# Gated DeltaNet gates worked out with tokens on the partitions, sums over tokens as TensorE products with masks

## The chip, the cores and the metric

The kernel runs on one core of a Trainium2 chip. The metric is the device time of one execution in microseconds; where several executions are shown, their median counts. A core has TensorE (PE, with its weight loads shown apart as PEld), VectorE (DVE), ScalarE (ACT), GpSimd (POOL) and SyncE (SP), which here issues all DMAs. PE multiplies into PSUM; DVE and ACT read PSUM and SBUF, POOL only SBUF.

## The reference, cut to what matters

A two-layer decoder trunk: layer 0 is a gated DeltaNet, layer 1 an RWKV-7 mixer. The prompt has 16 meta tokens and 1024 prompt tokens; besides it there are 8 sample sequences of 8 tokens. The change is in the gates of layer 0: beta and the log decay g, the cumulative sum of g within a chunk, and what follows from it.

```python
proj = xn @ w_in
qkv, z, b, a = proj[..., :c1], proj[..., c1:c2], proj[..., c2:c3], proj[..., c3:]
...
beta = jax.nn.sigmoid(b)
g = -jnp.exp(a_log.astype(jnp.float32)) * jax.nn.softplus(a + dt_bias)
...
gc = jnp.cumsum(g, axis=-1)
decay = jnp.exp(jnp.where(causal, gc[..., :, None] - gc[..., None, :], -jnp.inf))
...
L = jnp.where(strict, jnp.einsum('nbhik,nbhjk->nbhij', kb, k) * decay, 0.0)
A = L + jnp.eye(chunk, dtype=L.dtype)
sol = lax.linalg.triangular_solve(A, rhs, left_side=True, lower=True, unit_diagonal=True)
...
k_dec = k * jnp.exp(g_last[..., None] - gc)[..., None]
q_dec = q * jnp.exp(gc)[..., None]
...
S = S * jnp.exp(gl_c)[..., None, None] + jnp.einsum('bhck,bhcv->bhkv', kd_c, v_new)
```

There are 16 value heads, so b and a are 16 columns each of the input projection.

## The kernel before

**Tiling.** All 1104 tokens (64 sample tokens, 16 meta, 1024 prompt) go through together, as three segments of 384, 384 and 336 columns (`SEGS`), features on the partitions. For the recurrence, tokens are cut in nine groups of 128 (`tg` 0 to 8; group 0 holds the 8 sample sequences in its first 64 rows and a first prompt piece in its last 64). Products in layer 0 are made of three fp32r products (a high and a low part of each operand, `split` and `dense`); weights are loaded by SP, split by ACT (L87, high part) and POOL (L91, low part).

**Layer 0.** `input_norm` loads x, norms it and transposes it onto the features. `gates` projects b and a (L77, tile `d`, 64 columns of weights of which 32 are used). Then come eight head pairs j = 0 to 7. For each pair the projections run in the order of `ORDER`: k, the z of the pair before (x, y), q, and the two v (v, w). `conv` turns k, q, v into conv outputs: an ACT copy out of PSUM, one ACT tap and three DVE taps (L524), a tanh and a DVE product (L530). `gdn_prep` makes the scores K K^T (PE, tile `fsc`), scales them by the decays and bp (DVE L700 to L710), sends the 32x32 blocks through DRAM (`ltd`, L716) and inverts 72 blocks together on DVE in 31 steps of two instructions (`inverse32`, L571 and L573). `spread` sends the inverse through DRAM (`g_t`, `g_u`) to `T1n` and `TT`; the merges y32, u32, y64, u64 on PE (tiles `rY`, `rU`) put the blocks together. `gdn_recur` then runs over the nine groups.

**The order.** Within layer 0, PE and ACT follow an order written out by hand (`manual_schedule`); DVE, POOL and SP are put in order by a planner that simulates a time line. The hand-written order counts in slots: a slot is half a segment of one projection, 12 products on PE. Slot -24 is the first of dk of pair 0, slots -18 to -13 are dq. `self.at(u, f)` puts f behind the slot that lies before u: an event at -23.4 is issued behind slot -24. For pair 0: loads of E at -18.5 to -18.3, exps of E (ACT) from -16, scores at -15.2, -14.4 and -13.6, spread at -1, merges from 2.5 on. The gates are a generator: its first part (projection) runs ahead of the slots, and each `yield` is continued by one event.

**The gates before** (`gates_open`, `gates`, L317 to L404). Heads lie on partitions, 16 each, tokens along the row: `rows[0:16]` is beta, `rows[32:48]` the cumulative sum gc, `rows[64:80]` the rest of the chunk gd = gc at its end minus gc. Per segment: tanh of b, a plus the bias, |a|, exp (ACT and DVE, 16 lanes). Then over all 1104 columns: Ln, softplus, product with -exp(a_log), and the cumulative sum as a DVE scan (L373) with a mask `sm` that is 0 at the start of each chunk. The differences are three DVE subtractions (L379 to L382). The chunk decays exp(gc at the end) are made on 16 lanes (`egl`), written to DRAM (`dgl`, L387) and read back broadcast to 128 partitions (`eglb`, L388). gc goes to DRAM as `drow[j]` in eight DMAs (L393). Last, nine PE transposes (L74) in three batches bring beta, gc and gd onto token partitions, and DVE (L401, L402) and ACT fill `col`, whose four planes are beta, -gc, exp(gc) and exp(gd). These steps are events at -22.9, -19.4, -16.8, -16.7 and -16.6.

**Who uses them.** `decays` (L643 to L657) loads E (for the scores) and attn (for the outputs): gc of a pair's two heads and three groups, broadcast to 128 partitions, one DMA for each pair, segment and use, 48 in all (L647); POOL masks them (L651), ACT takes the exps with `col[..., 1, ...]` as bias. `gdn_prep`, `gdn_tokens`, `gdn_recur` and the sample steps read `col` and `eglb`.

Of the kernel before, what the change touches and what calls it, by code (L numbers as in the profile page):

```python
# [10 lines left out]
AF = mybir.ActivationFunctionType  # L11
ALU = mybir.AluOpType
# [3 lines left out]
NT = 1104  # L16
# [6 lines left out]
NEG = -1.0e30  # L23
# [13 lines left out]
class Builder:  # L37
# [277 lines left out]


    def gates_open(self, ctx):  # L317
        nc, i = self.nc, self.i
        W = i["gdn_w_in"][0]

        self.col = self.t(self.l0, [128, 9, 4, 16], "gcol")
        self.eglb = self.t(self.l0, [128, 16, 17], "eglb")
        self.bmask4 = self.t(self.l0, [64, 4], "bmask4")
        for g in (0, 1):
            nc.gpsimd.tensor_copy(self.bmask4[32 * g:32 * g + 32], self.bmask[32 * g:32 * g + 32, 4 * g:4 * g + 4])
        gp = self.gatep = ctx.enter_context(self.tc.tile_pool(name="gates", bufs=1, reuse_waits="tile"))
        t = self.t
        al = t(gp, [128, 2], "al")
        wz = t(gp, [128, 8, 64], "wz")
        nc.gpsimd.memset(wz, 0.0)  # L330
        wv = W[:, 6144:6176].rearrange("(k p) m -> p k m", p=128)
        nc.sync.dma_start(wz[:, :, 0:16], wv[:, :, 0:16])
        nc.sync.dma_start(wz[:, :, 32:48], wv[:, :, 16:32])
        rows = t(gp, [96, 1152], "rows")
        nc.vector.memset(rows, 0.0)
        g = t(gp, [48, 1152], "g")
        nc.vector.memset(g[32:48], 0.0)
        sm = t(gp, [48, 1152], "sm")
        nc.vector.memset(sm[32:48], 1.0)
        nc.gpsimd.memset(sm[32:48].rearrange("p (c k) -> p c k", k=128)[:, :, 0:1], 0.0)  # L340
        nc.gpsimd.memset(sm[32:48, 0:72].rearrange("p (c k) -> p c k", k=8)[:, :, 0:1], 0.0)
        self.gate_in = al, wz, rows, g, sm
        nc.sync.dma_start(al[32:48, 0:1], i["gdn_a_log"].rearrange("l h -> h l"))
        nc.sync.dma_start(al[32:48, 1:2], i["gdn_dt_bias"].rearrange("l h -> h l"))

    def gates(self, xh, xl):
        nc, i, t, gp = self.nc, self.i, self.t, self.gatep
        al, wz, rows, g, sm = self.gate_in
        nea = t(gp, [128, 1], "nea")
        self.act(nea[32:48], al[32:48, 0:1], AF.Exp)  # L350
        nc.vector.tensor_scalar(nea[32:48], nea[32:48], -1.0, None, op0=ALU.mult)
        whi = t(gp, [128, 8, 64], "whi2", dt=F32R)
        wlo = t(gp, [128, 8, 64], "wlo2", dt=F32R)
        self.split(wz, whi, wlo)
        w = ([whi[:, 0:4, :], whi[:, 4:8, :]], [wlo[:, 0:4, :], wlo[:, 4:8, :]])
        x = t(gp, [48, NT], "ax")
        y = t(gp, [48, NT], "ay")
        for s, (c0, n) in enumerate(SEGS):
            p = self.dense(w, 64, xh, xl, s)
            b = rows[0:16, c0:c0 + n]  # L360
            self.act(b, p[0:16, 0:n], AF.Tanh, scale=0.5)
            nc.vector.tensor_scalar(b, b, 0.5, 0.5, op0=ALU.mult, op1=ALU.add)
            xa, ya = x[32:48, c0:c0 + n], y[32:48, c0:c0 + n]
            self.act(xa, p[32:48, 0:n], AF.Identity, bias=al[32:48, 1:2])
            nc.vector.scalar_tensor_tensor(ya, xa, -1.0, xa, op0=ALU.mult, op1=ALU.max)
            self.act(ya, ya, AF.Exp, scale=-1.0)
        yield
        xa, ya = x[32:48], y[32:48]
        self.act(ya, ya, AF.Ln, bias=1.0)
        nc.vector.scalar_tensor_tensor(ya, xa, 0.0, ya, op0=ALU.max, op1=ALU.add)  # L370
        nc.vector.tensor_scalar(g[32:48, 0:NT], ya, nea[32:48], None, op0=ALU.mult)
        gc = rows[32:48]
        nc.vector.tensor_tensor_scan(gc, sm[32:48], g[32:48], 0.0, op0=ALU.mult, op1=ALU.add)  # L373
        yield
        gd = rows[64:80]
        c3 = lambda x: x.rearrange("p (c k) -> p c k", k=128)
        c8 = lambda x: x[:, 0:64].rearrange("p (c k) -> p c k", k=8)
        v, v8 = c3(gc), c8(gc)
        nc.vector.tensor_tensor(c3(gd)[:, 1:9], v[:, 1:9, 127:128].broadcast_to([16, 8, 128]), v[:, 1:9], op=ALU.subtract)  # L379
        nc.vector.tensor_tensor(c3(gd)[:, 0:1, 64:128], v[:, 0:1, 127:128].broadcast_to([16, 1, 64]), v[:, 0:1, 64:128],  # L380
                                op=ALU.subtract)
        nc.vector.tensor_tensor(c8(gd), v8[:, :, 7:8].broadcast_to([16, 8, 8]), v8, op=ALU.subtract)  # L382
        egl = t(gp, [48, 17], "egl")
        self.act(egl[32:48, 0:8].unsqueeze(2), v8[:, :, 7:8], AF.Exp)
        self.act(egl[32:48, 8:17].unsqueeze(2), v[:, :, 127:128], AF.Exp)
        dgl = self.dram([16, 17], "dgl")
        nc.sync.dma_start(dgl, egl[32:48])  # L387
        nc.sync.dma_start(self.eglb.rearrange("p h c -> p (h c)"),  # L388
                          dgl.rearrange("(o h) c -> o (h c)", o=1).broadcast_to([128, 272]))

        self.drow = self.dram([8, 9, 2, 128], "drow")
        for j in range(8):
            nc.sync.dma_start(self.drow[j].rearrange("t h k -> h t k"), c3(gc)[2 * j:2 * j + 2])  # L393
        for t3 in range(3):
            yield
            p = self.ps("f", 2)
            for k in range(3):
                self.transpose(p[:, 96 * k:96 * k + 96], rows[:, (3 * t3 + k) * 128:(3 * t3 + k + 1) * 128])
            pv = p[:, 0:288].rearrange("p (k x h) -> p k x h", k=3, h=16)
            c = self.col[:, 3 * t3:3 * t3 + 3]  # L400
            nc.vector.tensor_copy(c[:, :, 0, :], pv[:, :, 0, :])  # L401
            nc.vector.tensor_scalar(c[:, :, 1, :], pv[:, :, 2, :], -1.0, None, op0=ALU.mult)  # L402
# [240 lines left out]
    def decays(self, j, s, pool, tag, bufs):  # L643

        nc = self.nc
        E = self.t(pool, [128, 3, 2, 128], tag, bufs)
        nc.sync.dma_start(E.rearrange("p t h k -> p (t h k)"),  # L647
                          self.drow[j, 3 * s:3 * s + 3].rearrange("(o t) h k -> o (t h k)", o=1).broadcast_to([128, 768]))
        E6 = E.rearrange("p t h k -> p (t h) k")

        nc.gpsimd.affine_select(E6, E6, pattern=[[0, 6], [1, 128]], compare_op=ALU.is_ge, fill=NEG, base=0, channel_multiplier=-1)  # L651
        if s == 0:
            nc.gpsimd.memset(E6[0:64, 0:2, 64:128], NEG)
            for h in (0, 1):
                v = E6[0:64, h, 0:64].rearrange("p (b r) -> p b r", r=8)
                nc.gpsimd.affine_select(v, v, pattern=[[-8, 8], [0, 8]], compare_op=ALU.is_ge, fill=NEG, base=0, channel_multiplier=1)
        return E  # L657
# [263 lines left out]
    def gdn_events(self, G, open_, gate, swap):  # L921

        self.events = {}
        base = [-24]
        for j in range(8):
            base.append(base[j] + 6 * min(len(ORDER[j]), 6))
        first = [9, 43] + [base[j + 1] + 6 for j in range(2, 8)]
        for u in (-22.9, -19.4, -16.8, -16.7, -16.6):
            self.at(u, gate)
        self.at(-13, swap)  # L930
        for j in range(8):
            self.chain_events(j, G, first[j])
            self.front_events(j, G, base[j] if j else -24, first[j], first[j - 1] if j else None, open_)
# [1198 lines left out]
    def layer0(self, top, right, xa, xc):  # L2132
# [265 lines left out]
    def wave(self, zin, first, loaded_, stay, last, pool):  # L2398
# [23 lines left out]
        def norms(s):  # L2422
            x = self.sums_in(s)
            for _ in range(2 + s):
                yield
            yield from self.finish(s, x)

        jobs = [(gates, 32, -4.5, 14), (lambda: out(0, Z), 16, 14, 22), (lambda: out(1, DD), 16, 22, 30),
                (lambda: out(2, Z), 16, 30, 38), (lambda: out(3, DD), 16, 38, 46), (lambda: out(4, Z, None, range(6)), 12, 46, 52), (lambda: out(4, DD, x2, (6, 7)), 4, 52.1, 52.45),
                (lambda: out(5, DD, x2), 16, 52.1, 54.5), (lambda: out(6, DD, x2), 8, 54.6, 56), (lambda: self.finish_last(x2), 1, 56, 57)]  # L2430
# [121 lines left out]
```

## Time and profile before

| | us |
|---|---|
| median of three executions | 2184.01 (2181.36 to 2190.6) |
| the profiled execution | 2190.08 |
| its span | 2188.3 |
| granted TensorE clock, mean | 0.981 |

Which engine is busy when, in 40 slices of 54.7 us each (tenths; 9 is 90% or more), with the granted clock:

```profile
PE   5869899999999999999999999999898999999997
DVE  7967869788887979795334676757968657777755
ACT  5526466656565665656533365664746446777774
POOL 3423333334343333334231352343534344444444
PEclk9979999999999999999999999999999999999999
```

How to read the views used below. The page's first part gives the busy us of each engine, its share of the span and its instructions. A wait row names who waited for whom, the us in total, the number of waits and the longest. A row of a stretch gives start:end, its length, and the busy us of PE, PEld, DVE, ACT and POOL with instruction counts, then the granted clock, the DMA share and GB/s. A row of the time line gives the start, the us, the engine and line, and the operation with output<-input, and in brackets the idle time before it and who ended it. A grouped row gives the instructions of a line with their count, then busy us and mean ns, then the idle time before them. SPq rows are DMA issues.

### The profile page before, as it was taken

What the parts mean: (1) busy time and instruction counts of PE and PEld (TensorE: products, weight loads), DVE (VectorE), ACT (ScalarE), POOL (GpSimd) and SP (SyncE); (2) the same over time, 40 slices, a digit from 0 to 9 for tenths busy, and PEclk for the clock granted to TensorE, in tenths of its full rate; (3) what the DMA queues carried; (4) which work ended last, traced back from release to release, by engine and by line L of the source; (5) the groups of instructions that cost most, each with busy time, mean ns of one, the idle gap of its engine ahead of it and who ended that gap; (6) DMA issues with size and microseconds to landing.
All of it is one profiled execution on the core that took longest, in us unless ns stands there. A gap on an engine that the chain in (4) does not pass through costs nothing. (4 is left out here: it accounts for less than half of the span.)

```text
span 2188.3 us, 54818 instructions
## 1 busy us (share of the span) xinstructions
PE 2048.3 (94%) x20404; PEld 1905.8 (87%) x20404; DVE 1585.8 (72%) x4221; ACT 1290.9 (59%) x3761; POOL 841.2 (38%) x1125
## 2 busy tenths in 40 slices
PE   5869899999999999999999999999898999999997
PEld 5859899999999999998899999888898988888876
DVE  7967869788887979795334676757968657777755
ACT  5526466656565665656533365664746446777774
POOL 3423333334343333334231352343534344444444
PEclk9979999999999999999999999999999999999999
DMA  4423342424333333335345115655565476677764
GB/s 119 119 58 87 90 115 85 116 78 106 96 96 106 105 96 102 98 102 165 97 126 134 61 51 190 215 167 168 168 180 152 119 221 175 181 229 221 239 178 138
DMA packets 430661, 292.65 MB, mean 134 GB/s; under 512 B 147145, under 2 KB 412986, under 8 KB 430394
## 3 DMA queue, kind: packets, MB, share of 16 engines
q1 hardware_dynamic: 430394, 289.14, 46.0%
q8 instruction: 161, 2.64, 0.5%
q14 instruction: 106, 0.87, 0.1%
HBM read 197.68 MB, written 91.37 MB: 132 GB/s over the span
## 5 line engine op out<-in xcount | busy, mean ns | idle before, releaser
L91 POOL TENSOR_TENSOR wlo<-wraw,whi 128x512 fp32r<-128x512 f32 (+1 forms) x246 | 328.5, 1337 | 475.8 <-ACT whi L87 432.1
L77 PE MATMUL d<-xc,whi 128*128 128x384 f32 (+2 forms) x1006 | 279.1, 336 | 0.8 <-DVE xc L313 0.7
L524 DVE SCALAR_TENSOR_TENSOR cvy<-raw,cw,cvy 128x408 f32<-128x408 f32 (+2 forms) x288 | 189.1, 657 | 19.2 <-ACT cvy L63 17.8
L87 ACT CAST whi<-wraw 128x512 fp32r<-128x512 f32 (+1 forms) x246 | 149.9, 612 | 87.2 <-PE d L77 50.0
L77 PEld LDWEIGHTS d<-xc,whi 128*128 128x128 f32 (+1 forms) x1006 | 183.0, 189 | 3.4 <-DVE xc L313 1.1
L77 PE MATMUL d<-xc,wlo 128*128 128x384 f32 (+3 forms) x476 | 157.5, 339 | 3.8 <-POOL wlo L91 3.8
L77 PE MATMUL dz<-xc,whi 128*128 128x384 f32 (+1 forms) x480 | 153.7, 338 | 0.0
L77 PE MATMUL dv<-xc,whi 128*128 128x384 f32 (+1 forms) x480 | 152.2, 337 | 0.0
L77 PE MATMUL d<-xa,whi 128*128 128x384 f32 (+3 forms) x450 | 142.9, 341 | 8.4 <-ACT ev L2352 4.1
L63 ACT ACTIVATE o<-rA,gcol 128x128 f32<-128x128 f32 x128 | 42.2, 367 | 116.2 <-DVE S L903 116.0
L571 DVE TENSOR_TENSOR invtmp<-invA,invT 72x31 f32<-72x31 f32 (+15 forms) x248 | 101.8, 411 | 3.2
L77 PE MATMUL dv<-xa,whi 128*128 128x384 f32 (+1 forms) x288 | 99.0, 344 | 0.0
L77 PE MATMUL dz<-xa,whi 128*128 128x384 f32 (+1 forms) x288 | 98.5, 342 | 0.0
L77 PEld LDWEIGHTS d<-xc,wlo 128*128 128x128 f32 (+1 forms) x476 | 89.2, 189 | 7.9 <-POOL wlo L91 4.9
L77 PEld LDWEIGHTS d<-xa,whi 128*128 128x128 f32 (+1 forms) x450 | 84.3, 190 | 12.9 <-ACT ev L2352 4.4
L573 DVE TENSOR_TENSOR invT<-invT,invtmp 72x31 f32<-72x31 f32 (+15 forms) x248 | 92.7, 374 | 3.3
L77 PEld LDWEIGHTS dz<-xc,whi 128*128 128x128 f32 x480 | 89.3, 188 | 4.6 <-issue 4.5
L77 PEld LDWEIGHTS dv<-xc,whi 128*128 128x128 f32 x480 | 89.1, 188 | 1.4 <-issue 1.4
L77 PE MATMUL d<-xa,wlo 128*128 128x384 f32 (+3 forms) x252 | 84.8, 337 | 2.0 <-POOL wlo L91 2.0
L77 PE MATMUL dq<-xc,whi 128*128 128x384 f32 (+1 forms) x240 | 78.3, 343 | 3.0 <-ACT whi L87 3.0
L77 PE MATMUL dk<-xc,whi 128*128 128x384 f32 (+1 forms) x240 | 78.2, 346 | 0.0
L1333 DVE SCALAR_TENSOR_TENSOR mixs<-xb,pcol,mixs 128x320 f32<-128x320 f32 (+2 forms) x96 | 69.4, 733 | 5.0 <-ACT mixs L63 4.7
(523 smaller groups left out, 6821.9 us busy)
## 6 DMA issues: line engine op xcount, KB each, us to landing
wraw<-in_gdn_w_in SPq DMA_DIRECT2D x96, 256.0 KB
wraw<-in_rwkv_w_rkvz SPq DMA_DIRECT2D x80, 256.0 KB
Sb<-in_state_gdn SPq DMA_DIRECT2D x64, 256.0 KB
sldcak<-cakd SPq DMA_DIRECT2D x24, 576.0 KB
wraw<-in_rwkv_w_o SPq DMA_DIRECT2D x42, 256.0 KB
E<-drow SPq DMA_DIRECT2D x24, 384.0 KB
attn<-drow SPq DMA_DIRECT2D x24, 384.0 KB
wraw<-in_gdn_w_out SPq DMA_DIRECT2D x36, 256.0 KB
```

The costliest lines, as they stand in the source:

```text
L63: return self.nc.scalar.activation(out, in_, func, bias=bias, scale=scale, **kw)
L77: self.nc.tensor.matmul(out, lhsT, rhs, start=start, stop=stop)
L87: nc.scalar.copy(hi, x)
L91: e.tensor_tensor(lo, x, hi.bitcast(F32), op=ALU.subtract)
L524: nc.vector.scalar_tensor_tensor(y[0][:, 0:wd], raw[:, k:k + wd], cw[k], y[0][:, 0:wd], op0=ALU.mult, op1=ALU.add)
L571: nc.vector.tensor_tensor(tmp, A[:, j, j + 1:32].unsqueeze(2).broadcast_to([nb, n, m]), Tv[:, j, 0:m].unsqueeze(1).broadcast_to([nb, n, m] ...
L573: nc.vector.tensor_tensor(Tv[:, j + 1:32, 0:m], Tv[:, j + 1:32, 0:m], tmp, op=ALU.subtract)
L1333: nc.vector.scalar_tensor_tensor(x[:, f:], xb[:, 8 + a + f:8 + b], mu, x[:, f:], op0=ALU.mult, op1=ALU.add)
```

## The change

The gates are worked out with tokens on the partitions. The projection's 48 rows are copied out of PSUM once per segment; nine PE transposes put them on 128 partitions as [128, 9 groups, 48], and all elementwise work runs on [128, 9, 16]. The cumulative sum over a chunk's tokens is a PE product with a 0/1 mask `upto` (one mask for group 0 with its sample blocks, one for groups 1 to 8), the rest of the chunk a product with `past`. The chunk decays come out on all 128 partitions by a product of `ones` with g (for group 0, with g split by `part` into its nine chunks), so `dgl` goes. The DRAM rows `drow` get the layout [9, 16, 128] and are written by two DMAs from transposes of gc; `decays` reads them in three pieces per partition. `al` is loaded broadcast to 128 partitions. The masks are made by POOL at the start. The events of the gates become three, at -23.4, -21.4 and -20.4.

```diff
-        al = t(gp, [128, 2], "al")
+        al = t(gp, [128, 2, 16], "al")
...
-        rows = t(gp, [96, 1152], "rows")
-        nc.vector.memset(rows, 0.0)
-        g = t(gp, [48, 1152], "g")
-        nc.vector.memset(g[32:48], 0.0)
-        sm = t(gp, [48, 1152], "sm")
-        nc.vector.memset(sm[32:48], 1.0)
-        nc.gpsimd.memset(sm[32:48].rearrange("p (c k) -> p c k", k=128)[:, :, 0:1], 0.0)
-        nc.gpsimd.memset(sm[32:48, 0:72].rearrange("p (c k) -> p c k", k=8)[:, :, 0:1], 0.0)
-        self.gate_in = al, wz, rows, g, sm
-        nc.sync.dma_start(al[32:48, 0:1], i["gdn_a_log"].rearrange("l h -> h l"))
-        nc.sync.dma_start(al[32:48, 1:2], i["gdn_dt_bias"].rearrange("l h -> h l"))
+        for x, nm in enumerate(("gdn_a_log", "gdn_dt_bias")):
+            nc.sync.dma_start(al[:, x], i[nm].broadcast_to([128, 16]))
+        rows = t(gp, [48, 1152], "rows")
+        nc.gpsimd.memset(rows[:, NT:1152], NEG)
+
+        upto, past = [t(gp, [128, 128], f"upto{k}") for k in (0, 1)], [t(gp, [128, 128], f"past{k}") for k in (0, 1)]
+        for k in (0, 1):
+            for m, c, b in ((upto[k], 1, 0), (past[k], -1, -1)):
+                nc.gpsimd.memset(m, 1.0)
+                nc.gpsimd.affine_select(m, m, pattern=[[c, 128]], compare_op=ALU.is_ge, fill=0.0, base=b, channel_multiplier=-c)
+        nc.gpsimd.memset(upto[0][0:64, 64:128], 0.0)
+        nc.gpsimd.memset(past[0][64:128, 0:64], 0.0)
+        part = t(gp, [128, 9], "part")
+        nc.gpsimd.memset(part, 0.0)
+        nc.gpsimd.tensor_copy(part[0:64, 0:8], self.bmask[0:64])
+        nc.gpsimd.memset(part[64:128, 8:9], 1.0)
+        for m, c, b in ((upto[0], 1, 0), (past[0], -1, 7)):
+            v = m[0:64, 0:64].rearrange("p (b r) -> p b r", r=8)
+            nc.gpsimd.affine_select(v, v, pattern=[[-8 * c, 8], [0, 8]], compare_op=ALU.is_ge, fill=0.0, base=b, channel_multiplier=c)
+        self.gate_in = al, wz, rows, upto, past, part
 
...
-        nea = t(gp, [128, 1], "nea")
-        self.act(nea[32:48], al[32:48, 0:1], AF.Exp)
-        nc.vector.tensor_scalar(nea[32:48], nea[32:48], -1.0, None, op0=ALU.mult)
+        al, wz, rows, upto, past, part = self.gate_in
+        nea = t(gp, [128, 16], "nea")
+        self.act(nea, al[:, 0], AF.Exp)
+        nc.vector.tensor_scalar(nea, nea, -1.0, None, op0=ALU.mult)
...
-        x = t(gp, [48, NT], "ax")
-        y = t(gp, [48, NT], "ay")
         for s, (c0, n) in enumerate(SEGS):
             p = self.dense(w, 64, xh, xl, s)
-            b = rows[0:16, c0:c0 + n]
-            self.act(b, p[0:16, 0:n], AF.Tanh, scale=0.5)
-            nc.vector.tensor_scalar(b, b, 0.5, 0.5, op0=ALU.mult, op1=ALU.add)
-            xa, ya = x[32:48, c0:c0 + n], y[32:48, c0:c0 + n]
-            self.act(xa, p[32:48, 0:n], AF.Identity, bias=al[32:48, 1:2])
-            nc.vector.scalar_tensor_tensor(ya, xa, -1.0, xa, op0=ALU.mult, op1=ALU.max)
-            self.act(ya, ya, AF.Exp, scale=-1.0)
+            nc.scalar.copy(rows[:, c0:c0 + n], p[0:48, 0:n])
         yield
-        xa, ya = x[32:48], y[32:48]
-        self.act(ya, ya, AF.Ln, bias=1.0)
-        nc.vector.scalar_tensor_tensor(ya, xa, 0.0, ya, op0=ALU.max, op1=ALU.add)
-        nc.vector.tensor_scalar(g[32:48, 0:NT], ya, nea[32:48], None, op0=ALU.mult)
-        gc = rows[32:48]
-        nc.vector.tensor_tensor_scan(gc, sm[32:48], g[32:48], 0.0, op0=ALU.mult, op1=ALU.add)
+        col = self.col
+        p = self.ps("f", 2, "gt")
+        for k in range(9):
+            self.transpose(p[:, 48 * k:48 * k + 48], rows[:, 128 * k:128 * k + 128])
+        pv = p[:, 0:432].rearrange("p (k x) -> p k x", x=48)
+        b, x, y, g = [t(gp, [128, 9, 16], n) for n in ("gb", "gx", "gy", "g")]
+        nc.vector.tensor_tensor(x, pv[:, :, 32:48], al[:, 1].unsqueeze(1).broadcast_to([128, 9, 16]), op=ALU.add)
+        nc.vector.scalar_tensor_tensor(y, x, -1.0, x, op0=ALU.mult, op1=ALU.max)
+        self.act(y, y, AF.Exp, scale=-1.0)
+        self.act(b, pv[:, :, 0:16], AF.Tanh, scale=0.5)
+        self.act(y, y, AF.Ln, bias=1.0)
+        nc.vector.scalar_tensor_tensor(y, x, 0.0, y, op0=ALU.max, op1=ALU.add)
+        nc.vector.tensor_tensor(g, y, nea.unsqueeze(1).broadcast_to([128, 9, 16]), op=ALU.mult)
+        gs = t(gp, [128, 9, 16], "gs")
+        nc.vector.tensor_tensor(gs, g[:, 0].unsqueeze(1).broadcast_to([128, 9, 16]), part.unsqueeze(2).broadcast_to([128, 9, 16]), op=ALU.mult)
+        nc.vector.tensor_scalar(col[:, :, 0, :], b, 0.5, 0.5, op0=ALU.mult, op1=ALU.add)
         yield
-        gd = rows[64:80]
-        c3 = lambda x: x.rearrange("p (c k) -> p c k", k=128)
-        c8 = lambda x: x[:, 0:64].rearrange("p (c k) -> p c k", k=8)
-        v, v8 = c3(gc), c8(gc)
-        nc.vector.tensor_tensor(c3(gd)[:, 1:9], v[:, 1:9, 127:128].broadcast_to([16, 8, 128]), v[:, 1:9], op=ALU.subtract)
-        nc.vector.tensor_tensor(c3(gd)[:, 0:1, 64:128], v[:, 0:1, 127:128].broadcast_to([16, 1, 64]), v[:, 0:1, 64:128],
-                                op=ALU.subtract)
-        nc.vector.tensor_tensor(c8(gd), v8[:, :, 7:8].broadcast_to([16, 8, 8]), v8, op=ALU.subtract)
-        egl = t(gp, [48, 17], "egl")
-        self.act(egl[32:48, 0:8].unsqueeze(2), v8[:, :, 7:8], AF.Exp)
-        self.act(egl[32:48, 8:17].unsqueeze(2), v[:, :, 127:128], AF.Exp)
-        dgl = self.dram([16, 17], "dgl")
-        nc.sync.dma_start(dgl, egl[32:48])
-        nc.sync.dma_start(self.eglb.rearrange("p h c -> p (h c)"),
-                          dgl.rearrange("(o h) c -> o (h c)", o=1).broadcast_to([128, 272]))
-
-        self.drow = self.dram([8, 9, 2, 128], "drow")
-        for j in range(8):
-            nc.sync.dma_start(self.drow[j].rearrange("t h k -> h t k"), c3(gc)[2 * j:2 * j + 2])
-        for t3 in range(3):
-            yield
-            p = self.ps("f", 2)
-            for k in range(3):
-                self.transpose(p[:, 96 * k:96 * k + 96], rows[:, (3 * t3 + k) * 128:(3 * t3 + k + 1) * 128])
-            pv = p[:, 0:288].rearrange("p (k x h) -> p k x h", k=3, h=16)
-            c = self.col[:, 3 * t3:3 * t3 + 3]
-            nc.vector.tensor_copy(c[:, :, 0, :], pv[:, :, 0, :])
-            nc.vector.tensor_scalar(c[:, :, 1, :], pv[:, :, 2, :], -1.0, None, op0=ALU.mult)
-            self.act(c[:, :, 2, :], pv[:, :, 2, :], AF.Exp)
-            self.act(c[:, :, 3, :], pv[:, :, 4, :], AF.Exp)
+        flat = lambda a: a.rearrange("p k h -> p (k h)")
+        p = self.ps("f", 2, "gc")
+        for a, m in ((0, upto), (144, past)):
+            self.mm(p[:, a:a + 16], m[0], g[:, 0])
+            self.mm(p[:, a + 16:a + 144], m[1], flat(g[:, 1:9]))
+        c, d = (p[:, a:a + 144].rearrange("p (k h) -> p k h", h=16) for a in (0, 144))
+        gc = t(gp, [128, 9, 16], "gc")
+        nc.vector.tensor_copy(gc, c)
+        e = self.ps("m", 1, "ge")
+        self.mm(e[:, 0:144], self.ones, flat(gs))
+        self.mm(e[:, 144:272], self.ones, flat(g[:, 1:9]))
+        self.act(col[:, :, 1, :], c, AF.Identity, scale=-1.0)
+        self.act(self.eglb.rearrange("p h c -> p c h"), e[:, 0:272].rearrange("p (c h) -> p c h", h=16), AF.Exp)
+        self.act(col[:, :, 2, :], c, AF.Exp)
+        self.act(col[:, :, 3, :], d, AF.Exp)
+        yield
+        p = self.ps("f", 2, "gr")
+        self.transpose(p[:, 0:128], flat(gc[:, 0:8]))
+        self.transpose(p[0:16, 128:256], gc[:, 8])
+        r = t(gp, [128, 256], "gr")
+        nc.vector.tensor_copy(r[:, 0:128], p[:, 0:128])
+        nc.vector.tensor_copy(r[0:16, 128:256], p[0:16, 128:256])
+        self.drow = self.dram([9, 16, 128], "drow")
+        nc.sync.dma_start(self.drow[0:8].rearrange("t h k -> (t h) k"), r[:, 0:128])
+        nc.sync.dma_start(self.drow[8], r[0:16, 128:256])
...
         E = self.t(pool, [128, 3, 2, 128], tag, bufs)
-        nc.sync.dma_start(E.rearrange("p t h k -> p (t h k)"),
-                          self.drow[j, 3 * s:3 * s + 3].rearrange("(o t) h k -> o (t h k)", o=1).broadcast_to([128, 768]))
+        nc.sync.dma_start(E.rearrange("p t h k -> p t (h k)"),
+                          self.drow[3 * s:3 * s + 3, 2 * j:2 * j + 2].rearrange("(o t) h k -> o t (h k)", o=1).broadcast_to([128, 3, 256]))
...
-        for u in (-22.9, -19.4, -16.8, -16.7, -16.6):
+        for u in (-23.4, -21.4, -20.4):
```

More of the change, by code (lines that the diff above doesn't have):

```diff
@@ L317, in gates_open @@
     def gates_open(self, ctx):
-        nc, i = self.nc, self.i
+        nc, i, t = self.nc, self.i, self.t
         W = i["gdn_w_in"][0]
-        self.col = self.t(self.l0, [128, 9, 4, 16], "gcol")
-        self.eglb = self.t(self.l0, [128, 16, 17], "eglb")
-        self.bmask4 = self.t(self.l0, [64, 4], "bmask4")
+        self.col = t(self.l0, [128, 9, 4, 16], "gcol")
+        self.eglb = t(self.l0, [128, 16, 17], "eglb")
+        self.bmask4 = t(self.l0, [64, 4], "bmask4")
         for g in (0, 1):
@@ L326, in gates_open @@
         gp = self.gatep = ctx.enter_context(self.tc.tile_pool(name="gates", bufs=1, reuse_waits="tile"))
-        t = self.t
-        al = t(gp, [128, 2], "al")
+        al = t(gp, [128, 2, 16], "al")
         wz = t(gp, [128, 8, 64], "wz")
@@ L346, in gates @@
+        nc.gpsimd.memset(part[64:128, 8:9], 1.0)
[3 more added lines that the diff above has]
+        self.gate_in = al, wz, rows, upto, past, part
     def gates(self, xh, xl):
         nc, i, t, gp = self.nc, self.i, self.t, self.gatep
-        al, wz, rows, g, sm = self.gate_in
```

## The prediction

> **What bounds the kernel now.** I read the page's first part, then the table of waits for the first 300 us, then the stretches of the time around the gates.
>
> ```profile
> span 2188.3 us, 54818 instructions
> PE 2048.3 (94%) x20404; PEld 1905.8 (87%) x20404; DVE 1585.8 (72%) x4221; ACT 1290.9 (59%) x3761; POOL 841.2 (38%) x1125
> PE rY L77 <- DMA T1n<-g_t: 26.5, 3, 20.0
> PE dq L77 <- ACT whi L87: 3.0, 1, 3.0
> 46.00:56.00 10.00, 10.00 (x60) 9.46 (x59) 1.90 (x7) 4.88 (x8) 0.39 (x2) 1.00 0.03 7
> 56.00:62.00 6.00, 5.97 (x38) 5.65 (x36) 5.87 (x5) 3.04 (x5) 1.78 (x2) 1.00 0.17 44
> 62.00:70.00 8.00, 4.26 (x12) 3.87 (x13) 7.87 (x15) 2.80 (x7) 2.54 (x6) 0.63 0.31 70
> 70.00:77.00 7.00, 6.54 (x42) 6.26 (x42) 5.04 (x13) 5.23 (x19) 5.07 (x9) 0.94 1.06 302
> 77.00:98.00 21.00, 19.31 (x147) 18.26 (x146) 20.67 (x71) 11.78 (x33) 11.65 (x19) 1.00 0.41 104
> 98.00:124.00 26.00, 22.34 (x162) 20.95 (x160) 25.55 (x64) 11.99 (x34) 9.69 (x13) 1.00 0.24 66
> 124.00:137.00 13.00, 0.00 (x0) 0.00 (x0) 11.94 (x34) 0.00 (x0) 0.00 (x0) 0.56 0.10 28
> ```
>
> Over the whole span PE is the bound (94%). But in each stretch (after its length come the busy us of PE, PEld, DVE, ACT and POOL, then the granted clock) the first 137 us look otherwise. From 56 to 137 us, DVE is busy for all but about 4 of 81 us, and from 124 to 137 us PE does nothing at all. The waits say for what: one wait of 20.0 us, by the merge products rY, for T1n. That is the inverse of head pair 0, which DVE works out.
>
> ```profile
> 97.65 0.17 DVE L571 TENSOR_TENSOR invtmp<-invA,invT 72x31 f32<-72x31 f32 x1
> 135.86 0.19 DVE L573 TENSOR_TENSOR invT<-invT,invtmp 72x31 f32<-72x31 f32 x1
> 136.07 0.27 SPq L744 DMA_DIRECT2D g_t<-invT  x1
> ```
>
> So the inverse runs on DVE from 97.65 to 136.05, then goes through DRAM, and PE resumes. PE's queue is in hand-written order, so nothing of PE gets past that point. **What the gates cost is what they hold back the end of this inverse**; a microsecond of PE saved ahead of it only lengthens the wait. From there on the work is the same in both kernels, and a shift of this end is carried through to the end of the span.
>
> **The change part by part.** *DVE, out.*
>
> ```profile
> L373 DVE TENSOR_TENSOR_SCAN rows<-sm,g 16x1152 f32<-16x1152 f32 x1 | 2.5, 2547 | 0.0
> L370 DVE SCALAR_TENSOR_TENSOR ay<-ax,ay 16x1104 f32<-16x1104 f32 x1 | 1.3, 1299 | 3.6 <-ACT ay L63 3.6
> L382 DVE TENSOR_TENSOR rows<-rows 16x64 f32<-16x64 f32 x1 | 1.3, 1280 | 0.0
> L379 DVE TENSOR_TENSOR rows<-rows 16x1024 f32<-16x1024 f32 x1 | 1.2, 1218 | 0.0
> L371 DVE TENSOR_SCALAR g<-ay,nea 16x1104 f32<-16x1104 f32 x1 | 0.8, 784 | 0.0
> L401 DVE COPY gcol<-f 128x48 f32<-128x48 f32 x3 | 0.6, 207 | 1.0 <-PE f L74 1.0
> L402 DVE TENSOR_SCALAR gcol<-f 128x48 f32<-128x48 f32 x3 | 0.6, 197 | 0.0
> L380 DVE TENSOR_TENSOR rows<-rows 16x64 f32<-16x64 f32 x1 | 0.2, 208 | 0.0
> ```
>
> With tokens along the row, 16 lanes carry 1104 elements each. These rows are all in the saturated stretch: 2.5 + 1.3 + 1.3 + 1.2 + 0.8 + 0.6 + 0.6 + 0.2 = 8.5 us. L382 has 64 elements as L380 has, which took 0.2; its other 1.1 us are a hold-up that I expect the next instruction to inherit. I count 7.4 us. The elementwise work on each segment (L362, L365) and the three memsets lie before 56 us, where DVE waits for others; I count them at nothing, under the cover of the input norm and of PE, which is full from 46 to 56.
>
> *DVE, in.* With tokens on 128 partitions a gate is 9x16 = 144 columns. The added work is x, |x|, softplus, g, gs, beta, the copy gc and two copies for the DRAM rows: nine instructions. The trace has none at 144 columns; the nearest are these:
>
> ```profile
> 133.30 0.30 DVE L571 TENSOR_TENSOR invtmp<-invA,invT 72x135 f32<-72x135 f32 x1
> 123.58 0.41 DVE L571 TENSOR_TENSOR invtmp<-invA,invT 72x256 f32<-72x256 f32 x1
> ```
>
> I take 0.30 each, nearest in width: 2.7 us. With L401's 0.207 (48 columns) below and 0.41 (256 columns) above, it is 1.9 to 3.7. Net: 7.4 - 2.7 = **4.7 us less DVE work**, bounds 3.7 and 6.6 (8.5 - 1.9).
>
> *The same sum by dates*, since less work helps only if the conv and the scores come early enough to fill DVE.
>
> ```profile
> 50.49 0.44 ACT L63 ACTIVATE rows<-d 16x336 f32<-16x336 f32 x1 [4.94 <-PE d L77]
> L74 PE MATMUL f<-ident,rows 96*128 96x96 f32 x9 | 1.5, 316 | 0.5 <-ACT gcol L63 0.5
> L77 PE MATMUL fsc<-K 128*128 128x128 f32 x18 | 2.6, 280 | 1.1 <-DVE E L710 1.1
> 74.04 0.83 PE L77 MATMUL fsc<-K 128*128 128x128 f32 x6
> 76.67 0.28 DVE L700 SCALAR_TENSOR_TENSOR fsc<-fsc,ident 128x128 f32<-128x128 f32 x1
> L63 ACT ACT_TABLE_LOAD x2 | 2.6, 1283 | 0.0
> ```
>
> The last segment is out of PSUM at 50.9. Nine transposes (1.5 us, as now) end at 52.4. A slot is 12 products, 2.0 us at the 60 in 10 us of the second fence row above. Slots -23 and -22 end at 56.4. Meanwhile x, |x|, Exp, Tanh, one table load of 1.28, Ln, softplus, g, gs: 8 x 0.3 + 1.3 = 3.7 us, ready near 56.1, so the products with masks hardly wait. Six of them at 2.6/18 are 0.9 us: 57.3. Slot -21, then transposes of gc: 59.7. Then five slots (-20 to -16): the first scores at 69.7 on PE instead of 74.04. They come after Q's first segment on DVE, near 71.3 instead of 76.67: 5.4 us earlier, and from there DVE has the same work. Two sums, 4.7 and 5.4: I take **5.0**.
>
> The 3.0 us that PE now waits for weights behind ACT, which waits for a conv behind the scan, goes too. Granted clock after it: 0.63 over 62 to 70. The next one late is DVE itself, with the scores. The Trainium skill ("TensorE: Matmul & The Clock Gate", Part 1) has the clock halved after an idle window of about 3.4 us; the trace agrees about the direction, and removing that wait is worth no more than the dates above already hold.
>
> *ACT.* Three long passes over 16 lanes and an Ln over 1104 columns become three copies and seven instructions of 144 to 272 columns. ACT is busy for under two thirds of any stretch up to 70: nothing, as long as Ln's chain is short. The two table loads stay. The Trainium skill ("ScalarE: Activation LUTs", What ACT_TABLE_LOAD costs) puts a switch at 2.66 us with its drain, which would make PE wait some 1.4 us at the masks and the gain 3.6; the row above has 1283 ns, and I keep to it.
>
> *POOL and SP at the start.*
>
> ```profile
> 7.92 0.10 POOL L340 MEMSET sm<- 16x9 f32 x1 [4.38 <-DVE sm L339]
> 11.43 0.71 POOL L103 TENSOR_TENSOR rs<-ss,cvals 128x2 f32<-128x2 f32 x1 [3.40 <-DVE ss L292]
> 1.26 0.29 POOL masks.py:199 TENSOR_SCALAR_AFFINE_SELECT ident<-ident 128x128 f32<-128x128 f32 x1
> 6.45 4.45 SPq L343 DMA_DIRECT2D al<-in_gdn_a_log x1
> 11.40 2.83 SPq L264 DMA_DIRECT2D x<-in_x_prompt  x6
> ```
>
> Some 16 small POOL instructions for the masks, at most 0.29 each: under 4.6 us, beside 7.8 us in which POOL now waits. Nothing; without that cover rs and the input norm would be late by up to 1 us. The two al loads go from 16 rows to 128 rows, ahead of the x tiles in SP's queue: 0 to 1 us late, taken as nothing against L362 and L365.
>
> *DMAs.* Ten small issues (eight drow, dgl, eglb) become two, and the bounce for eglb goes.
>
> ```profile
> 62.68 1.84 SPq L393 DMA_DIRECT2D drow<-rows  x6
> 67.06 1.37 SPq L647 DMA_DIRECT2D E<-drow  x3
> 73.88 0.91 POOL L651 TENSOR_SCALAR_AFFINE_SELECT E<-E 128x768 f32<-128x768 f32 x1 [0.25 <-DMA E<-drow]
> E<-drow SPq DMA_DIRECT2D x24, 384.0 KB
>   POOL attn L651: 55.3, 17
> ```
>
> From the first drow issue to E is 4.4 us now. With two issues at 60.5 and about 1.4 us of round trip E is issued near 62 and lands by 62 + 6.8 (67.06 to 73.88) = 69, just ahead of the scores. In all 48 loads of E and attn each partition's row now comes in three pieces of 1 KB instead of one of 3 KB. Bytes are the same; below, no cost; above, a third rival.
>
> **The rivals.**
> 1. *The gate chain blocks PE and ACT.* Both queues are in written order: behind the mask products stand all of dk and dq, behind Exp and Ln the raw copies and conv taps. The gain is gone if g comes 5 us late (61 us). For it: a transposing round trip through four engines. Against: in the stretch 46 to 56, DVE is 81% idle and POOL 96%. Time: 2184, no change.
> 2. *More than the sum.* The norm ahead of the gates ends earlier too, since L362, L365 (3.2 us of DVE together) and some 3 us of ACT leave it, and all the upper bounds hold: 6.6 + 3.2 + 3 = 12.8 us at most, 2171. Against: PE is full from 46 to 56, so an earlier norm mostly changes the order of what it does.
> 3. *Slower: the loads in three pieces.* Place: SP's queue to POOL's select of attn, where POOL already waits 55.3 us in 17 waits. If three pieces cost three times the engine time (384 KB at the 302 GB/s of 70 to 77 is 1.3 us), each load lands 2.6 us later; it decides once ACT's exps, which stand in written order before PE's scores, run out of slack. Price: 17 x 2.6 = 44 us at most, half of it likely: 2184 - 5 + 22 = 2201. Against: bytes are the same, and outside 70 to 77 the DMA share in the stretches above is under a half.
> 4. *DVE's, POOL's and SP's orders are the planner's.* Other dates early on can reshuffle them far behind, for better or worse. A collision like L382's costs 1.1 us; ten more or fewer over the eight head pairs are 11 us, and the time 2168 or 2190.
>
> **How the numbers follow.** The profiled execution is 2190.08 us (span 2188.3 and 1.8 around it), 6 us above the median 2184.01 (2181.36 to 2190.6), so 2185 in its terms and 2184 - 5 = **2179** in the median's. The sum and its bounds (2177 to 2181, to 2184 with half of the dates lost) 0.55; rival 1, 0.18; rival 2, 0.10; rival 3, 0.05; rival 4, 0.12, half on each side. A measurement of this kernel tells 0.5% (11 us) from no change. Under 2173: 0.14 (0.08 of rival 2, the better half of 4). Over 2195: 0.07 (rival 3, and a third of the worse half of 4). Range: from 2170 (rival 2) to 2190 (rival 1 with runs that spread like those shown, and the worse half of 4); likeliest case alone 2174 to 2184.
>
> **What would show it.** The wait of rY for T1n ends near 136, not 141; the last inverse step ends near 131; no wait of PE of 3 us for whi near 62; first scores near 70; DVE's work on gcol, g and rows under 3 us; E lands before ACT's exps ask for it. I am wrong if PE waits for the mask products over 2 us, if DVE idles over 8 us between 56 and 131, or if POOL's waits for attn grow.

## The result, and the profile after

| | before | after |
|---|---|---|
| median us (4 runs each) | 2184.31 (2181.36 to 2190.6) | 2308.64 (2300.49 to 2311.49) |
| profiled execution / its span | 2190.08 / 2188.3 | 2300.49 / 2298.7 |
| granted clock, mean | 0.981 | 0.963 |

The ratio is 1.0559, 95% interval 1.0524 to 1.0594: **slower by 5.6%**, where 2179 was forecast.

The page of after, first part and slices (57.5 us each):

```profile
span 2298.7 us, 54823 instructions
PE 2082.9 (91%) x20418; PEld 1934.0 (84%) x20418; DVE 1555.9 (68%) x4209; ACT 1287.8 (56%) x3753; POOL 823.2 (36%) x1139
PE   6769899899898989989989999989999999999997
PEclk9879999899999999999999999989999999999998
```

PE has about the same work, but its busy time is 34.6 us longer (2082.9 - 2048.3) and its idle time 75.8 us (215.8 - 140.0); together they are the 110.4 us by which the span grew. The 8s in PE's row come again and again up to slice 21, and once more in slice 27: this is no event at the start, though the change's work lies in the first 60 us. The stretches of before, then of after:

```profile
300.00:400.00 100.00, 98.13 (x890) 95.02 (x890) 86.70 (x249) 61.86 (x206) 35.30 (x53) 1.00 0.40 109
400.00:500.00 100.00, 98.65 (x725) 94.05 (x724) 82.64 (x243) 61.24 (x203) 38.27 (x54) 1.00 0.35 95
```

```profile
300.00:400.00 100.00, 90.75 (x618) 86.24 (x617) 71.02 (x221) 54.39 (x184) 30.12 (x46) 0.93 0.40 86
400.00:500.00 100.00, 85.19 (x725) 80.80 (x724) 59.41 (x179) 53.70 (x176) 29.20 (x44) 0.91 0.41 85
```

PE loses 7 and 13 us of each 100, and along with its gaps the granted clock falls from 1.00 to 0.91 to 0.93. The longer busy time fits that: from 300 to 1000 us a `dz` product of 384 columns (high half of the weights, `xc`) takes 367 ns on average, before 346. The last two figures say more: the DMA engines are no less busy than before (0.40 and 0.41 for 0.40 and 0.35), but move fewer GB/s (86 and 85 for 109 and 95). The table of waits, rows of before and then of after:

```profile
POOL E L651 <- DMA E<-drow: 8.6, 5, 3.4
PE rY L77 <- DMA T1n<-g_t: 27.6, 5, 20.0
PE rA L77 <- DVE S L903: 2.8, 7, 0.7
```

```profile
POOL attn L656 <- DMA attn<-drow: 83.0, 15, 11.4
POOL E L656 <- DMA E<-drow: 63.5, 16, 7.2
PE rY L77 <- DMA T1n<-g_t: 36.9, 13, 20.0
PE dz L77 <- POOL wlo L91: 33.4, 5, 7.5
PE dv L77 <- POOL wlo L91: 11.9, 1, 11.9
PE rA L77 <- DVE S L908: 28.1, 20, 3.8
```

PE's new idle time is 75.8 us net. Four rows add 79.9: 33.4 before `dz` and 11.9 before `dv`, waits that before did not have, 25.3 more before `rA`, 9.3 more before `rY`; some small waits went. POOL's waits for E and attn grew with them: 63.9 us before (8.6 + 55.3), 146.5 after. The time line shows how a load gets to PE, here at pair 3's start:

```profile
425.38 0.39 SPq L652 DMA_DIRECT2D E<-drow  x1
...
426.34 0.43 SPq L652 DMA_DIRECT2D E<-drow  x1
...
428.30 1.66 SPq L652 DMA_DIRECT2D E<-drow  x1
...
443.93 0.86 POOL L656 TENSOR_SCALAR_AFFINE_SELECT E<-E 128x768 f32<-128x768 f32 x1 [3.30 <-DMA E<-drow]
...
444.80 1.26 POOL L91 TENSOR_TENSOR wlo<-wraw,whi 128x512 fp32r<-128x512 f32 x1
...
446.12 0.69 PE L77 MATMUL dz<-xc,wlo 128*128 128x384 f32 x1 [7.08 <-POOL wlo L91]
```

The last load of E, issued at 428.30, reaches POOL at 443.93. POOL works in order, so the low part of the z weights (`wlo`), which has nothing to do with E, comes behind it, and PE stands still for 7.08 us. The row names `wlo`; the cause is the load ahead of it. Four more such waits, of 5.35 to 7.51 us, come at the later pairs.

At the start, where the prediction looked, the time line of after has these rows, and behind them stands before's row of `rY`:

```profile
53.13 0.31 DVE L382 TENSOR_TENSOR gs<-g,part 128x144 f32<-128x144 f32 x1
56.46 0.30 DVE L392 COPY gc<-fgc 128x144 f32<-128x144 f32 x1
59.47 1.43 SPq L652 DMA_DIRECT2D E<-drow  x3
67.05 0.87 POOL L656 TENSOR_SCALAR_AFFINE_SELECT E<-E 128x768 f32<-128x768 f32 x1 [3.55 <-DMA E<-drow]
69.25 0.29 DVE L705 SCALAR_TENSOR_TENSOR fsc<-fsc,ident 128x128 f32<-128x128 f32 x1
71.92 0.86 POOL L656 TENSOR_SCALAR_AFFINE_SELECT E<-E 128x768 f32<-128x768 f32 x1 [2.44 <-DMA E<-drow]
77.23 0.86 POOL L656 TENSOR_SCALAR_AFFINE_SELECT E<-E 128x768 f32<-128x768 f32 x1 [4.37 <-DMA E<-drow]
85.91 0.86 POOL L656 TENSOR_SCALAR_AFFINE_SELECT attn<-attn 128x768 f32<-128x768 f32 x1 [7.53 <-issue]
88.05 0.69 PE L77 MATMUL dv<-xa,wlo 128*128 128x384 f32 x1 [11.94 <-POOL wlo L91]
91.18 1.30 DVE L529 SCALAR_TENSOR_TENSOR cvy<-raw,cw,cvy 128x336 f32<-128x336 f32 x1 [8.17 <-ACT cvy L63]
147.27 0.31 PE L77 MATMUL rY<-T1n,E 32*32 32x32 f32 x2 [20.05 <-DMA T1n<-g_t]
```

```profile
141.32 0.31 PE L77 MATMUL rY<-T1n,E 32*32 32x32 f32 x2 [20.04 <-DMA T1n<-g_t]
```

The gates are done on time and the first score is there at 69.25. But the three loads of E, issued together from 59.47, land some 5 us apart: 384 KB in 5 us is about 79 GB/s. ACT's exps wait for them, the conv taps behind the exps too, DVE sits idle for 8.17 us at 91, and `rY` starts at 147.27 instead of 141.32. The first loads of attn are issued from 73.89, behind those of E; POOL's select of attn comes at 85.91 after 7.53 us without work, the low part of the v weights stands behind it, and PE waits 11.94 us before `dv`, its longest new wait.

### The profile page after: what moved, and what is told of

It is laid out like the page before. It is cut to its first block, busy times and chain, and to the rows that moved or that the text cites. A ratio compares the mean times of both kernels' runs of the same rounds, so it can differ in the third digit from the quotient of the medians.

```text
span 2298.7 us, 54823 instructions
## 1 busy us (share of the span) xinstructions
PE 2082.9 (91%) x20418; PEld 1934.0 (84%) x20418; DVE 1555.9 (68%) x4209; ACT 1287.8 (56%) x3753; POOL 823.2 (36%) x1139
## 5 line engine op out<-in xcount | busy, mean ns | idle before, releaser
L529 DVE SCALAR_TENSOR_TENSOR cvy<-raw,cw,cvy 128x408 f32<-128x408 f32 (+2 forms) x288 | 184.5, 641 | 48.3 <-ACT cvy L63 46.9
L77 PE MATMUL dz<-xc,whi 128*128 128x384 f32 (+1 forms) x480 | 159.1, 349 | 0.0
L77 PE MATMUL dz<-xc,wlo 128*128 128x384 f32 (+1 forms) x192 | 67.7, 353 | 33.4 <-POOL wlo L91 33.4
L77 PE MATMUL rA<-S,K 128*128 128x128 f32 x256 | 49.7, 296 | 38.1 <-DVE S L908 28.1
```

The costliest lines, as they stand in the source:

```text
L77: self.nc.tensor.matmul(out, lhsT, rhs, start=start, stop=stop)
L529: nc.vector.scalar_tensor_tensor(y[0][:, 0:wd], raw[:, k:k + wd], cw[k], y[0][:, 0:wd], op0=ALU.mult, op1=ALU.add)
```

## The experiments

The theory after this look: the loads of E and attn from the new `drow` layout [9, 16, 128], three runs of 1 KB that lie 8192 B apart, cost everything. The rivals: it is the number of runs; it is the gates' own work, or the order that the planner made of it. All ratios are to the kernel before on the same chip (medians there 2186.4, 2182.64 and 2182.63 in the three groups of runs).

**One run instead of three, gates as in after.** gc is copied in the order (pair, group, head), so that a load is one run of 3 KB again.

```diff
-        gc = t(gp, [128, 9, 16], "gc")
-        nc.vector.tensor_copy(gc, c)
+        gc = t(gp, [128, 8, 9, 2], "gc")
+        nc.vector.tensor_copy(gc.rearrange("p j t h -> p t j h"), c.rearrange("p t (j h) -> p t j h", h=2))
...
-        self.drow = self.dram([9, 16, 128], "drow")
+        self.drow = self.dram([8, 9, 2, 128], "drow")
...
-                          self.drow[3 * s:3 * s + 3, 2 * j:2 * j + 2].rearrange("(o t) h k -> o t (h k)", o=1).broadcast_to([128, 3, 256]))
+                          self.drow[j, 3 * s:3 * s + 3].rearrange("(o t) h k -> o (t h k)", o=1).broadcast_to([128, 768]))
```

> The changed kernel with one thing undone: gc is put in the order (pair, group, head) before its transposes, so that drow is [8, 9, 2, 128] again and each partition's row of E and attn is one run of 3 KB. Theory L (the loads of E and attn in three runs cost the time): the loss goes and the front stays early, 2177 us (2170 to 2184), and the loads of E for pair 0 land within about 6 us, as before the change. Theory G (the new chain of the gates itself costs it, through PE's and ACT's written order): still 2290 to 2310 us.

Measured: 2180.16 (12 runs), ratio 0.9969 (0.9954 to 0.9983). With the gates of after and the loads of before the kernel is faster than before, by 6 us.

**The other half: before, with only the layout and the loads of after.**

```diff
-        self.drow = self.dram([8, 9, 2, 128], "drow")
+        self.drow = self.dram([9, 16, 128], "drow")
...
-                          self.drow[j, 3 * s:3 * s + 3].rearrange("(o t) h k -> o (t h k)", o=1).broadcast_to([128, 768]))
+                          self.drow[3 * s:3 * s + 3, 2 * j:2 * j + 2].rearrange("(o t) h k -> o t (h k)", o=1).broadcast_to([128, 3, 256]))
```

> The kernel before with one thing of the change alone: drow is [9, 16, 128], and E and attn are loaded in three runs of 1 KB per partition, 8 KB apart; the gates stay as they were. Theory L: 2184 + 125 + some 6 us (the gates' own gain, that the changed kernel has) = 2305 to 2325 us. Theory G: 2184 us.

Measured: 2312.15, ratio 1.0553 (1.0513 to 1.0593): +126 us, the whole loss, with the old gates. The gates are out of it, and the planner's order of them too.

**Three runs, at other distances.** Two heads of padding put the runs 9216 B apart; a layout [8, 9, 272] puts them 1088 B apart. The cut shows the first.

```diff
-        self.drow = self.dram([9, 16, 128], "drow")
+        self.drow = self.dram([9, 18, 128], "drow")
...
```

> The changed kernel with drow padded to [9, 18, 128]: still three runs of 1 KB per partition, but 9216 bytes apart instead of 8192. Theory L has two forms. L1, the number of runs: runs of 1 KB cost more wherever they lie, so 2295 to 2310 us as the changed kernel. L2, where they lie: runs 8192 bytes apart get in each other's way in DRAM, so 9216 bytes apart gives 2177 us (2170 to 2190). Theory G: 2300 us.

> The changed kernel with drow as [8, 9, 272], of which 256 are used: three runs of 1 KB per partition, 1088 bytes apart, so nearly one stretch of memory. L1 (the number of runs): 2295 to 2310 us. L2 (8192 bytes apart is what hurts): 2178 us (2170 to 2190). Theory G: 2300 us.

Measured: 2182.65 (10 runs), ratio 0.9981 (0.9962 to 0.9999), at 9216 B; 2188.67 (10 runs), 1.0010 (0.9994 to 1.0026), at 1088 B, which writes `drow` with one DMA more. Three runs cost at most a little: nothing at 9216 B, and at 1088 B 0.4% against the kernel with one run, part of which may be the extra write (not pursued). It is the 8192 B between them that cost. The queue rows of the pages, after and then the kernel with 9216 B (packets, MB, share of 16 engines):

```profile
q1 hardware_dynamic: 442746, 289.02, 47.4%
```

```profile
q1 hardware_dynamic: 442750, 289.03, 46.3%
```

The packets are as many, 12288 more than the 430458 with one run (48 loads x 128 rows x 2), and the bytes the same. The Trainium skill ("DMA: Bandwidth & Descriptors", Why small descriptors are slow) puts a fixed cost of about 3 cycles beside the 32-byte beats of each packet; by that, an estimate, three packets of 1 KB would take 105 cycles to 99 of one of 3 KB. No run here can show this: the 48 loads are 18.9 of the 289 MB, so 6% of their time would be 0.2 points of the share, and the kernel with one run has 46.3%, the one with earlier scores and the same loads 45.8%.

**E alone, attn alone.** `drow` as in the first experiment, and a second copy of it in the layout of after, from which one of the two is loaded.

```diff
+        self.drow8 = self.dram([9, 16, 128], "drow8")
+        nc.sync.dma_start(self.drow8.rearrange("t (j h) k -> j t (h k)", h=2), self.drow.rearrange("j t h k -> j t (h k)"))
...
+        if tag == "attn":
+            nc.sync.dma_start(E.rearrange("p t h k -> p t (h k)"),
+                              self.drow8[3 * s:3 * s + 3, 2 * j:2 * j + 2].rearrange("(o t) h k -> o t (h k)", o=1).broadcast_to([128, 3, 256]))
...
```

> As the run with one run of 3 KB, but a second copy of gc in DRAM has the changed layout, and attn alone is loaded from it, in three runs 8192 bytes apart; E keeps one run. If the harm goes by way of POOL's order (a late attn holds up all that stands behind its select), attn alone gives most of it, over 2250 us. If it goes by way of E, scores and inverse, attn alone gives little, under 2200 us. If it is only the DMA engines' time that is taken from other loads, half: 2230 to 2250 us.

> The other half: E alone in three runs 8192 bytes apart, attn in one run. By POOL's order with attn as the culprit: under 2210 us. By E, scores and inverse: over 2260 us, and the wait for T1n of pair 0 ends 8 to 12 us later than with one run. By the DMA engines' time: 2230 to 2250 us.

Measured: attn alone 2237.04, ratio 1.0252 (1.0231 to 1.0274); E alone 2235.57 (single executions from 2219.11 to 2241.5), 1.0218 (1.017 to 1.0267). About half each; against the 0.9969 of one run they add up to 0.0532 of after's 0.0590. The second copy is one DMA more at the start, and with E alone it moves the first issue of E to 63.62. The waits tell the two ways to PE apart, attn alone first, then E alone:

```profile
PE rY L77 <- DMA T1n<-g_t: 35.2, 13, 20.2
PE rA L77 <- DVE S L916: 25.7, 21, 3.2
PE dv L77 <- POOL wlo L91: 2.9, 1, 2.9
```

```profile
POOL E L664 <- DMA E<-drow: 49.6, 12, 7.2
PE dz L77 <- POOL wlo L91: 31.1, 5, 6.8
PE dv L77 <- POOL wlo L91: 7.2, 2, 5.2
PE rY L77 <- DMA T1n<-g_t: 28.3, 5, 20.1
PE rA L77 <- DVE S L916: 3.7, 7, 1.1
```

E alone brings the waits of `dz` (31.1 of after's 33.4) and 7.2 us before `dv`, and hardly any of the others; attn alone those of `rA` and `rY`, 2.9 before `dv`, and none of `dz`. A late E mostly stops the weights on POOL; a late attn mostly stops the recurrence. Half each is also what was expected if slow loads only took the DMA engines' time from others; the rows of waits speak for the two ways, the times alone don't decide it.

**Half the distance, and 512 B more.** Layouts [2, 9, 8, 128] and [9, 17, 128]: 4096 B and 8704 B.

> The changed kernel with drow as [2, 9, 8, 128]: three runs of 1 KB, 4096 bytes apart. If any power of two from 4096 on is bad: 2240 to 2310 us. If 8192 and its multiples alone are bad (of three runs 4096 apart the first and third are 8192 apart): between, 2200 to 2260 us. If only all three on the same 8192 count: 2178 us (2170 to 2190).

> The changed kernel with drow padded to [9, 17, 128]: three runs of 1 KB, 8704 bytes apart, which is 512 more than 8192. If memory is shared out in pieces of 1 KB that come round every 8192 bytes, half of each run falls on the next piece, the fullest piece serves 1.5 of 3 KB, some 170 GB/s: 2180 to 2195 us, with E of pair 0 landing 2 to 3 us apart. If any offset will do: 2170 to 2185 us, as with 9216. If the pieces are 2 KB or more: over 2230 us.

Measured: 2198.06, ratio 1.0069 (1.0048 to 1.0091), at 4096 B; 2200.55, 1.0086 (1.0066 to 1.0106), at 8704 B. Both lie between, and a little outside of what was expected of runs that share an 8192 B period (2200 to 2260 and 2180 to 2195).

**One run at a time, and one run three times.** Is it that three places far apart disturb each other, or that one place of 1 KB gives too little? First, after's layout with three DMAs of one run for each load. Then after with the middle group's run read three times; the decays of the two other groups are left out there.

```diff
-        nc.sync.dma_start(E.rearrange("p t h k -> p t (h k)"),
-                          self.drow[3 * s:3 * s + 3, 2 * j:2 * j + 2].rearrange("(o t) h k -> o t (h k)", o=1).broadcast_to([128, 3, 256]))
+        for tt in range(3):
+            nc.sync.dma_start(E[:, tt].rearrange("p h k -> p (h k)"),
+                              self.drow[3 * s + tt, 2 * j:2 * j + 2].rearrange("(o h) k -> o (h k)", o=1).broadcast_to([128, 256]))
```

> The changed layout (8192 bytes apart), but each load is three DMAs of one run, one after the other, so that the 128 partitions read mostly one run at a time. If the runs get in each other's way when they are read in turn: 2178 to 2200 us. If a run of 1 KB in that layout is slow by itself: 2290 to 2320 us.

```diff
-                          self.drow[3 * s:3 * s + 3, 2 * j:2 * j + 2].rearrange("(o t) h k -> o t (h k)", o=1).broadcast_to([128, 3, 256]))
+                          self.drow[3 * s + 1:3 * s + 2, 2 * j:2 * j + 2].rearrange("(o t) h k -> o t (h k)", o=1).broadcast_to([128, 3, 256]))
...
```

> The changed kernel, but each load of E and attn reads the run of 1 KB of the middle group three times instead of those of its three groups (and the exps take that group's bias), so that the decays of the other two groups are left out. Theory R (one stretch of 1 KB of DRAM gives only so much, some 85 GB/s, when 16 DMA engines read it at once, and runs 8192 bytes apart count as one stretch): 2290 to 2320 us, and the three loads of E of pair 0 land about 5 us apart. Theory C (three rows 8192 bytes apart disturb each other): there is one row only, so 2170 to 2190 us.

Measured: 2260.49, ratio 1.0360 (1.0336 to 1.0384), and 2291.49, 1.0501 (1.0481 to 1.052). With only one place read, nothing is left to disturb it, and it is nearly as slow as after: **one stretch of 1 KB, read for 128 partitions, is slow by itself**, and three stretches 8192 B apart are no faster than one. Three DMAs lie between the two values expected, and why they lose 48 us less than after is open; pair 0's E lands no sooner in them (78.08).

The same 8 us at the start, with the three loads of E issued at 59.4 to 60.6 in all of these kernels, show it as a rate (last column, all DMA of the core). In this order, each from its kernel's stretches: after, the same run three times, 4096 B, 8704 B, 9216 B:

```profile
60.00:68.00 8.00, 7.93 (x47) 7.61 (x47) 6.45 (x11) 4.36 (x10) 3.17 (x6) 1.00 0.75 74
```

```profile
60.00:68.00 8.00, 7.92 (x47) 7.60 (x47) 5.69 (x11) 4.82 (x12) 2.92 (x6) 1.00 0.56 71
```

```profile
60.00:68.00 8.00, 7.93 (x47) 7.61 (x46) 7.09 (x11) 4.92 (x13) 4.72 (x10) 1.00 0.67 130
```

```profile
60.00:68.00 8.00, 7.93 (x47) 7.61 (x47) 6.49 (x11) 4.85 (x12) 4.66 (x10) 1.00 0.66 153
```

```profile
60.00:68.00 8.00, 7.93 (x48) 7.61 (x47) 7.58 (x10) 3.91 (x9) 6.80 (x14) 1.00 1.02 277
```

If addresses 8192 B apart share one source, 4096 B leave two places, of which one gives two thirds of the bytes (1.5 x 74 = 111), 8704 B spread three runs over 2 KB (2 x 74 = 148 at best), and 9216 B give three places (3 x 74 = 222). Measured: 130, 153 and 277, the loads that follow included, with issues up to 1.2 us apart. The order agrees, the sizes only roughly: POOL takes up the third load of E 10.18 us after the first in after (67.05, 77.23), 5.30 us at 4096 B (65.50, 70.80) and 5.53 at 8704 B (65.53, 71.06), so there these two are not told apart, nor are they by their times. A period of 4096 B would have given 74 at 4096 B and falls. That the memory is divided in this way is an inference and not shown.

**Can the earlier gates give more?** The kernel with one run, pair 0's exps and scores a slot earlier.

```diff
-            ed, ee, es = [-18.5, -18.4, -18.3], [-16, -15.2, -14.4], [-15.2, -14.4, -13.6]
+            ed, ee, es = [-18.5, -18.4, -18.3], [-17.2, -16.2, -15.2], [-16.2, -15.2, -14.2]
```

> The run with one run of 3 KB, and for pair 0 the exps of E and the scores one slot (2 us) earlier in PE's and ACT's written order, since E lands before they ask for it. If DVE's work decides the end of the inverse, the scores come 2 us earlier and the end by 0 to 2 us: 2175 to 2178 us, 0 to 2 us below the run with one run. If E or K come too late for the earlier place, PE waits and it is 1 to 3 us slower than that.

Measured: 2176.07 (12 runs), ratio 0.9968 (0.9956 to 0.9981). Not told apart from one run's 0.9969. Both beat before and after.

## Why the prediction was wrong

**The step that failed** is the last one under the DMAs: "In all 48 loads of E and attn each partition's row now comes in three pieces of 1 KB instead of one of 3 KB. Bytes are the same; below, no cost". Below was indeed possible: with pieces 9216 B apart they cost nothing, at 1088 B at most 0.4%. But where the pieces lie was not asked at all, and in the layout of the diff they lie 16 x 128 x 4 = 8192 B apart. That costs 126 us with the old gates, 128 (2308.64 - 2180.16, of two groups of runs) with the new.

**Rival 3** had the place (SP's queue, POOL's select, ACT's exps), and neither the price nor the reason. It priced pieces by their number, 2.6 us later for each load; a load took about 5 us instead of 1.3, 3.7 more, for a reason that is not the number. And it counted only the 17 waits for attn that were there before: E, with 8.6 us of waits, looked safe and makes half of the loss, as its loads, once slow, come in line ahead of POOL's weights. Its argument against, a DMA share under a half, was beside the point: in the stretches above the share hardly moved, while the rate fell. The nearest row was at hand: 302 GB/s while E was loaded, from runs of 3 KB. The trace of before has one load whose 128 rows come from 1 KB: `eglb` from `dgl`, 136 KB out of 1088 bytes, issued at 66.67. From 68.0 to 68.5 the DMAs moved 85 GB/s there at a share of 0.81, a us later 303 at 1.08; half a us is too short to prove a rate, but it was a hint, and the upper bound of 44 us had no row under it.

Two of the prediction's three signs of being wrong came: POOL's waits for attn grew (55.3 to 83.0), and DVE idled for 19 us between 56 and 131. The third did not: PE did not wait for the mask products.

**The rest of the sum** is tested by the kernel with one run:

```profile
67.81 0.85 POOL L658 TENSOR_SCALAR_AFFINE_SELECT E<-E 128x768 f32<-128x768 f32 x1
70.56 0.29 DVE L707 SCALAR_TENSOR_TENSOR fsc<-fsc,ident 128x128 f32<-128x128 f32 x1
137.83 0.31 PE L77 MATMUL rY<-T1n,E 32*32 32x32 f32 x2 [20.05 <-DMA T1n<-g_t]
```

- *DVE's new work*: nine instructions at 0.30 were forecast; in after they took 0.27 to 0.31 each, 2.7 us together. Right.
- *First scores near 71.3 on DVE*: 69.25 in after, 70.56 here. Right, and a little better, as g was ready at 53 and not at 56: rival 1, a gate chain that blocks PE, falls.
- *PE's wait of 3.0 us for `whi`*: gone; the granted clock from 62 to 70 is 1.00 in after and here, where before had 0.63.
- *E lands by 69*: with one run its last select began at 67.81 without a wait; in after at 77.23.
- *The end of rY's wait near 136*: 137.83 here, 134.94 with 9216 B, 147.27 in after. *That such a shift is carried to the end*: 3.5 us earlier here with 6 us of gain, 6.4 earlier at 9216 B with 4 (2182.65 to 2186.4): right within some 3 us, each date being that of one execution. The forecast 5.0 stands between the two.
- *Rival 2* (13 us) would be a ratio of 0.994, below the intervals of one run, 9216 B and the earlier scores; in *rival 4* the planner's new dates, present in the kernel with one run, made no loss.
- The clock was counted only for one wait. From 300 to 1100 us it was 0.91 to 0.97 in after, where before had 1.00, and PE's busy time grew by 34.6 us on top of the idle time. The Trainium skill ("TensorE: Matmul & The Clock Gate", Part 1), drawn on there, speaks of an idle window of some 3.4 us that halves the clock; gaps of 3 to 8 us such as those at 346 (3.85), 410 (3.52) and 446 (7.08) agree with that direction.

So the forecast's own terms held, and the one term that it took as nothing, with rival 3's chance at 0.05, was 25 times their sum (126 to 5).

## What to carry to other kernels

When a layout in DRAM changes, work out the distance between the pieces of each load and how many different bytes it reads, not only the number of pieces and bytes; a small row that is broadcast to 128 partitions is the case to look at. If 8192 bytes come out, pad: here [9, 18, 128] instead of [9, 16, 128] was worth 126 us. 4096 bytes cost 0.7%; other powers of two were not run. And price a late load by what stands behind it in the in-order queue of the engine that waits, not by the waits that are there today.

## What the runs showed of the hardware

While broadcast loads of 384 KB came from three 1 KB runs each, the core's DMAs moved 71 to 74 GB/s when the runs were one place or lay 8192 B apart, 130 with 4096 B, 153 with 8704 B, and 277 with 9216 B. The busy share of the DMA engines fell far less, from 1.02 at 9216 B to 0.75 at 8192 B and 0.56 with the one place. The Trainium skill ("DMA: Bandwidth & Descriptors", Latency and other measured facts) tells of rows at large powers of two: there the rate was 207 GB/s at a pitch of 512 KiB and 103 at 4 MiB, padding the latter by 4 KiB brought it back, and a clash of memory channels is suspected. The remedy agrees here, with 1 KB of padding; the size does not, as 8 KB was enough to lose three quarters of the rate, in loads whose 128 rows are all the same bytes.
